# Residuals added straight from the two halves of a product's tile, and mixer products in pairs of 256 and 512 columns, in a fp32 decoder trunk

## The chip, the core and the metric

The kernel runs on one core of one Trainium2 chip. The metric is the device time of one execution, in microseconds; of three runs the median counts. The engines that matter here are TensorE (PE: matrix products; PEld is its loading of weights), VectorE (DVE), ScalarE (ACT) and SyncE (SP), which issues the DMAs. Each engine works through its own list of instructions in order, and waits there until what an instruction needs has been signalled by others.

## The reference

Two macaron layers on x of 256 tokens by 1024 features, in fp32; six sub-layers s = 0 to 5 follow each other:

```python
x = x + 0.5 * (1.0 + mod[:, 0, 2]) * swiglu(pre(x, 0), ffn_wi[l, 0], ffn_wo[l, 0])
h = pre(x, 1)                       # rmsnorm, scale and shift
y = hgrn2_mixer(...) if kind == 0 else diff_attention_mixer(...)   # ends in o @ w_out
x = x + (1.0 + mod[:, 1, 2]) * y
x = x + 0.5 * (1.0 + mod[:, 2, 2]) * swiglu(pre(x, 2), ffn_wi[l, 1], ffn_wo[l, 1])
```

So s = 0, 2, 3, 5 are SwiGLU feed-forward parts (1024 to 2 x 2816 and back), s = 1 is the HGRN2 mixer and s = 4 the differential attention. After every sub-layer a gate per feature multiplies its output, and the sum with x is the new x: this is the residual that the change touches.

## The kernel before

**Layout.** x is held transposed in SBUF, as `xT` of 128 partitions x 8 chunks x 256 tokens; chunk d holds features 128 d to 128 d + 127. Weights come from HBM in blocks of up to 1 MB (`raw`, three buffers, DMAs issued by SP in a fixed order, up to four blocks ahead). Each block is split into a high part on ACT (`whi`, L231) and the rest on DVE (`wlo`, L232), two instructions each, up to two blocks ahead of its use; inputs are split likewise (`xh`/`xl`, `hx`, `a`, `yh`/`yl`). A product of fp32 precision is then the sum of three products in PE's fast type: high x high, high x low and low x high.

**Two forms of a product.** `mm3` (L349) issues the three as three matmuls of 256 columns into one 256-wide sum (L351 to L353). `mm2` (L355) issues low-weight x high-input as 256 columns (L359) and high-weight x [high|low input] as one matmul of 512 columns (L360), into a tile of two halves whose sum is the result:

```python
PE.matmul(acc[:, :S], wl, x2[:, 0], ...)                              # L359
PE.matmul(acc, wh, x2.rearrange("p a s -> p (a s)"), ...)             # L360
```

`joined` (L362) adds the halves: ACT copies the right one to SBUF (L365, tile `post`), DVE adds the left one to it (L366). Products land in PSUM tiles `mm` of 512 columns; five buffers rotate, so a tile's first matmul waits until the tile five before it has been read.

**The output products.** A feed-forward part ends in `out_product`: chunks are taken two by two, each with 22 k-steps of `mm2`, then `residual(s, d, joined(acc))`. A mixer ends in `mixer_out`: 8 k-steps (one for each head's `yh`, `yl`) of `mm3` for each chunk. The first six steps of chunks 0 to 3 are fill for PE while the heads are still worked on; when the last head is done, steps 6 and 7 of these follow, then chunks 4 to 7 whole.

**The tail of a sub-layer.** `residual` is one instruction on DVE (L504, xT = mm x gate + xT), and then, unless it is the last sub-layer, `scaled_chunk` prepares the next sub-layer's input: ACT makes `xh` (L301), DVE `xl` (L302), ACT the square `sq`, and DVE adds it to `ss` (L313). After chunk 7's `ss`, a matmul with ones (L327, `finish_norm`) sums over partitions; ACT makes `rstd` of it. Meanwhile `in_first` multiplies the next sub-layer's first weights with the unnormed `xh`, `xl` chunks as they come (L351 to L353, 258 columns: two carry the shift), in several tiles at once, and applies `rstd` later. In the last sub-layer a DMA stores each chunk in place of that.

**Order.** The program is written in one order, and a scheduler then sets the order of each engine's list by costs of its own; a change at one place can move instructions around it.

Of the kernel before, what the change touches and what calls it, by code (L numbers as in the profile page):

```python
# [10 lines left out]
F32 = mybir.dt.float32  # L11
F32R = mybir.dt.float32r
I32 = mybir.dt.int32
U32 = mybir.dt.uint32
AF = mybir.ActivationFunctionType
ALU = mybir.AluOpType
AX = mybir.AxisListType

P = 128
S = 256  # L20
# [4 lines left out]
H = 8  # L25
# [75 lines left out]
def trunk(ctx: ExitStack, tc, xT_in, c_in, vecs, positions, lam_in, kc_in, ada_w, ffn_wi, ffn_wo,  # L101
# [348 lines left out]

    def mixer_out(s, yh, yl, late):

        ws = [get((s, "out", d)) for d in range(2)]
        todo = [(w, c * P) for w in ws for c in range(2)]
        acc = []
        for w, c0 in todo:
            acc.append(mm_tile())
            for k in range(H - 2):
                mm3(acc[-1][:, :S], w, k, c0, yh[k], yl[k], k == 0, False)
                if k == H // 2 - 2:  # L460
                    yield
            yield
        while late:
            yield
        shift_cols(s + 1)
        for d in range(KD):
            if d < 4:
                for k in (H - 2, H - 1):
                    mm3(acc[d][:, :S], todo[d][0], k, todo[d][1], yh[k], yl[k], False, k == H - 1)
                residual(s, d, acc[d])  # L470
                continue
            w = get((s, "out", d // 2))
            t = mm_tile()
            for k in range(H):
                mm3(t[:, :S], w, k, (d % 2) * P, yh[k], yl[k], k == 0, k == H - 1)
            residual(s, d, t)
# [26 lines left out]
    def residual(s, d, acc):  # L503
        V.scalar_tensor_tensor(out=xT[:, d], in0=acc[:, :S], scalar=mod_a["mod_g", s][:, d:d + 1], in1=xT[:, d],  # L504
                               op0=ALU.mult, op1=ALU.add)
        if s + 1 < NSUB:
            scaled_chunk(s + 1, d)
        else:
            nc.sync.dma_start(out=out[d * P:(d + 1) * P, :], in_=xT[:, d])
# [5 lines left out]
    def out_product(s, ws_of, K, y2):  # L515

        for dp in range(4):
# [10 lines left out]
            for c in range(2):  # L528
                residual(s, dp * 2 + c, joined(acc[c]))

# [40 lines left out]
    def hgrn2(s):  # L571
        with tc.tile_pool(name="hg", bufs=2, reuse_waits="tile") as hp, \
# [12 lines left out]
            V.tensor_scalar(out=lb1, in0=lb, scalar1=-1.0, scalar2=1.0, op0=ALU.mult, op1=ALU.add)  # L585
            yh = [yp.tile([P, S], F32R, name=f"yh{h}") for h in range(H)]
            yl = [yp.tile([P, S], F32R, name=f"yl{h}") for h in range(H)]

# [16 lines left out]
            def fill():  # L605
                for p in range(4):
# [24 lines left out]
                    for c in range(2):  # L631
                        sl = slice(c * S, (c + 1) * S)
                        active.append(lag(STAG * c, core)(2 * p + c, qg[:, sl], k_[:, sl], lf[:, sl], v[:, :, c],
                                           qg[:, 2 * S + c * S:2 * S + (c + 1) * S]))
                yield from mixer_out(s, yh, yl, active)

            def core(h, q, k_, lf, v, g):
# [94 lines left out]
                for t in range(2):  # L732
# [3 lines left out]
                                       op0=ALU.mult, op1=ALU.mult)  # L736
                split(yh[h], yl[h], rs)

# [59 lines left out]
    def diff_attention(s):  # L798
        with tc.tile_pool(name="at", bufs=2, reuse_waits="tile") as hp, \
# [14 lines left out]
            V.tensor_scalar(out=slg, in0=vec[:, V_SL:V_SL + 1], scalar1=1.0 - LAMBDA_INIT, scalar2=None, op0=ALU.mult)  # L814
            yh = [yp.tile([P, S], F32R, name=f"byh{h}") for h in range(H)]
            yl = [yp.tile([P, S], F32R, name=f"byl{h}") for h in range(H)]
            scale = DH ** -0.5

            def fill():
                pre = in_first(s, [(s, "in", 0, 1), (s, "in", 0, 0)])  # L820
                rs = [{} for _ in range(4)]
                for n, (p, st) in enumerate(B_ORDER):
# [21 lines left out]
                    if not st:  # L844
                        for c in range(2):
                            active.append(lag(STAGA * c, core)(2 * p + c, r, c))
                yield from mixer_out(s, yh, yl, active)

# [44 lines left out]
            def core(h, r, c):  # L893
# [59 lines left out]
                for t in range(2):  # L953
                    PE.transpose(pn[:, t * P:(t + 1) * P], on[:, t * P:(t + 1) * P], ident)
                A.activation(out=yh[h], in_=pn[:, :S], func=AF.Copy, scale=slg)
                V.scalar_tensor_tensor(out=yl[h], in0=pn[:, :S], scalar=slg, in1=yh[h].bitcast(F32),
                                       op0=ALU.mult, op1=ALU.subtract)
# [163 lines left out]
```

## Time and profile before

| | us |
|---|---|
| median of three runs | 1062.84 |
| lowest and highest of the three | 1062.73, 1063.62 |
| the profiled execution's own time | 1065.88 |
| the span of that profile | 1064.1 |

| engine | busy us | share of the span | instructions |
|---|---|---|---|
| PE | 1042.3 | 98% | 7200 |
| DVE | 882.3 | 83% | 1761 |
| ACT | 662.8 | 62% | 1258 |
| POOL | 3.8 | 0% | 20 |

A share is an average over the whole span. Whether time can be won at one place depends on which engine is waited for there. Times within the span count from its start. An instruction's duration on PE or DVE is longer than the distance to the next one's start where the two overlap, so costs in a row are read from starts. The profile's rows join instructions of one kind that follow each other (x3), with the time from the first's start to the last's end.

### The profile page before, as it was taken

How to read it: one execution, taken by the hardware profiler on the slowest of the kernel's cores; microseconds unless marked ns; L12 is line 12 of the kernel's file. 1: busy time of each engine (PE TensorE's matmuls, PEld its weight loads, DVE VectorE, ACT ScalarE, POOL GpSimd, SP SyncE). 2: the span in 40 equal slices, each digit the busy share in tenths (PEclk: the TensorE clock that was granted, in tenths of full speed). 3: DMA queues.
4: the chain of work that ended last, by engine and by line, in shares of the span. 5: the costliest groups of instructions: out<-in, count | busy, mean ns of one | idle time of the engine just before them, and what ended most of it. 6: DMA issues, size and time to landing. Idle time of an engine off the chain costs nothing.

```text
span 1064.1 us, 18510 instructions
## 1 busy us (share of the span) xinstructions
PE 1042.3 (98%) x7200; PEld 931.9 (88%) x7200; DVE 882.3 (83%) x1761; ACT 662.8 (62%) x1258; POOL 3.8 (0%) x20
## 2 busy tenths in 40 slices
PE   8999999998999999999999999999999999999998
PEld 6788888897898898888889888888999999888887
DVE  6899888699897699998668999976899979887653
ACT  5666655586876675656446556654678786565541
POOL 0000000000000000000000000000000000000000
PEclk9999999999999999999999999999999999999999
DMA  9988788566764158887654888985466725766560
GB/s 357 356 285 294 266 309 284 179 243 231 259 248 170 50 193 307 311 321 273 219 193 160 317 312 322 336 292 194 165 241 249 261 86 198 283 227 214 190 209 20
DMA packets 41160, 256.03 MB, mean 241 GB/s; under 512 B 4721, under 2 KB 7025, under 8 KB 13426
## 3 DMA queue, kind: packets, MB, share of 16 engines
q1 hardware_dynamic: 41074, 254.87, 66.7%
q8 instruction: 56, 0.92, 0.3%
q14 instruction: 30, 0.25, 0.1%
HBM read 253.80 MB, written 1.05 MB: 240 GB/s over the span
## 4 chain that ended last, share of the span: by engine, by line
PE 84%; DVE 7%; DMA 5%; ACT 4%; issue 1%; SPq 0%; DVEq 0%
PE mm L360 41%; PE mm L359 21%; PE mm L351 5%; PE mm L352 5%; PE mm L353 5%; DMA rawa<-in_ada_w_dram 3%; PE mm L420 2%; PE mm L418 1%; PE mm L419 1%; DVE rawa L180 1%; DVE wlo L232 1%; DMA raw<-in_a_w_in_dram 1%; ACT whi L231 1%; DMA raw<-in_ffn_wi_dram 1%; ACT L337 1%
## 5 line engine op out<-in xcount | busy, mean ns | idle before, releaser
L232 DVE TENSOR_TENSOR wlo<-raw,whi 128x1024 fp32r<-128x1024 f32 (+1 forms) x336 | 394.1, 1197 | 88.3 <-ACT whi L231 87.4
L231 ACT ACTIVATE whi<-raw 128x1024 fp32r<-128x1024 f32 (+1 forms) x336 | 335.0, 1032 | 118.3 <-issue 47.5
L360 PE MATMUL mm<-hx,whi 128*128 128x512 f32 x1152 | 407.2, 397 | 0.0
L359 PE MATMUL mm<-hx,wlo 128*128 128x256 f32 x1152 | 323.9, 281 | 0.5 <-DVE post L399 0.5
L360 PEld LDWEIGHTS mm<-hx,whi 128*128 128x128 f32 x1152 | 216.5, 188 | 53.0
L360 PE MATMUL mm<-a,whi 128*128 128x512 f32 x704 | 247.3, 393 | 0.0
L359 PEld LDWEIGHTS mm<-hx,wlo 128*128 128x128 f32 x1152 | 216.3, 188 | 1.5 <-PE aux L1001 0.8
L359 PE MATMUL mm<-a,wlo 128*128 128x256 f32 x704 | 199.1, 283 | 0.0
L360 PEld LDWEIGHTS mm<-a,whi 128*128 128x128 f32 x704 | 132.2, 188 | 30.5
L180 DVE CUSTOM_DVE_ANT_0 rawa<-rawa,cact 128x1024 f32<-128x1024 f32 x128 | 154.6, 1222 | 3.3 <-DMA rawa<-in_ada_w_dram 3.1
L365 ACT ACTIVATE post<-mm 128x256 f32<-128x256 f32 x176 | 67.3, 383 | 128.7 <-PE mm L360 127.2
L359 PEld LDWEIGHTS mm<-a,wlo 128*128 128x128 f32 x704 | 132.4, 188 | 0.0
L366 DVE TENSOR_TENSOR post<-mm,post 128x256 f32<-128x256 f32 x176 | 73.7, 423 | 34.2 <-ACT post L365 33.4
L353 PE MATMUL mm<-xh,wlo 128*128 128x258 f32 x288 | 81.2, 283 | 0.0
L352 PE MATMUL mm<-xl,whi 128*128 128x258 f32 x288 | 81.0, 283 | 0.0
L351 PE MATMUL mm<-xh,whi 128*128 128x258 f32 x288 | 80.8, 285 | 0.0
L418 PE MATMUL mm<-whi,hx 128*128 128x256 f32 x208 | 59.8, 287 | 0.0
L420 PE MATMUL mm<-wlo,hx 128*128 128x256 f32 x208 | 59.3, 285 | 0.0
L419 PE MATMUL mm<-whi,hx 128*128 128x256 f32 x208 | 58.8, 283 | 0.0
L512 ACT ACTIVATE a<-us 128x256 fp32r<-128x256 f32 x88 | 34.9, 412 | 32.5 <-DVE us L560 28.9
L352 PEld LDWEIGHTS mm<-xl,whi 128*128 128x128 f32 x288 | 54.5, 189 | 0.2
L353 PEld LDWEIGHTS mm<-xh,wlo 128*128 128x128 f32 x288 | 54.4, 189 | 0.1
(226 smaller groups left out, 1444.4 us busy)
## 6 DMA issues: line engine op xcount, KB each, us to landing
raw<-in_ffn_wi_dram SPq DMA_DIRECT2D x84, 1024.0 KB, 4.8
rawa<-in_ada_w_dram SPq DMA_DIRECT2D x64, 1024.0 KB, 4.9
raw<-in_ffn_wo_dram SPq DMA_DIRECT2D x32, 1024.0 KB, 5.0
raw<-in_a_w_in_dram SPq DMA_DIRECT2D x16, 1024.0 KB, 4.8
raw<-in_ffn_wo_dram SPq DMA_DIRECT2D x16, 768.0 KB, 4.2
raw<-in_b_w_in_dram SPq DMA_DIRECT2D x12, 1024.0 KB, 4.7
rawa<-in_ada_w_dram SPq DMA_DIRECT2D x16, 512.0 KB, 7.6
wq<-in_ffn_wi_dram SPq DMA_DIRECT2D x16, 256.0 KB, 7.6
```

Of the source, the lines that this page charges most:

```text
L180: V.tensor_tensor_reduce(out=self.raw[:, d], in0=self.raw[:, d], in1=cact, scale=1.0, scalar=0.0, op0=ALU.mult, op1=ALU.add, accum_out=sum ...
L231: pin(A.activation(out=self.hi[:, sl], in_=self.raw[:, sl], func=AF.Copy))
L232: pin(V.tensor_tensor(out=self.lo[:, sl], in0=self.raw[:, sl], in1=self.hi[:, sl].bitcast(F32), op=ALU.subtract))
L351: PE.matmul(acc, wh, rh, start=start, stop=False)
L352: PE.matmul(acc, wh, rl, start=False, stop=False)
L353: PE.matmul(acc, wl, rh, start=False, stop=stop)
L359: PE.matmul(acc[:, :S], wl, x2[:, 0], start=start, stop=False, skip_group_check=True)
L360: PE.matmul(acc, wh, x2.rearrange("p a s -> p (a s)"), start=False, stop=stop, skip_group_check=True)
L366: V.tensor_tensor(out=t, in0=acc[:, :S], in1=t, op=ALU.add)
L418: PE.matmul(acc, xh_, wh, start=k == 0, stop=False)
L419: PE.matmul(acc, xl_, wh, start=False, stop=False)
L420: PE.matmul(acc, xh_, wl, start=False, stop=k == KD - 1)
```

## The change

The residual becomes two instructions on DVE for every chunk: xT gets gate x right half added, then gate x left half, both read from PSUM. `joined` is no longer called by `out_product` (it stays in the other products that use it). The mixers' `y` of a head is one tile of two halves, and `mixer_out` uses `mm2` in place of `mm3`.

```diff
-    def mixer_out(s, yh, yl, late):
+    def mixer_out(s, y2, late):
@@
-                mm3(acc[-1][:, :S], w, k, c0, yh[k], yl[k], k == 0, False)
+                mm2(acc[-1], w, k, c0, y2[k], k == 0, False)
@@
-                    mm3(acc[d][:, :S], todo[d][0], k, todo[d][1], yh[k], yl[k], False, k == H - 1)
+                    mm2(acc[d], todo[d][0], k, todo[d][1], y2[k], False, k == H - 1)
@@
-                mm3(t[:, :S], w, k, (d % 2) * P, yh[k], yl[k], k == 0, k == H - 1)
+                mm2(t, w, k, (d % 2) * P, y2[k], k == 0, k == H - 1)
@@
     def residual(s, d, acc):
-        V.scalar_tensor_tensor(out=xT[:, d], in0=acc[:, :S], scalar=mod_a["mod_g", s][:, d:d + 1], in1=xT[:, d],
-                               op0=ALU.mult, op1=ALU.add)
+
+        for part in (acc[:, S:], acc[:, :S]):
+            V.scalar_tensor_tensor(out=xT[:, d], in0=part, scalar=mod_a["mod_g", s][:, d:d + 1], in1=xT[:, d],
+                                   op0=ALU.mult, op1=ALU.add)
@@
-                residual(s, dp * 2 + c, joined(acc[c]))
+                residual(s, dp * 2 + c, acc[c])
@@
-                split(yh[h], yl[h], rs)
+                split(y2[h][:, 0], y2[h][:, 1], rs)
@@
-                A.activation(out=yh[h], in_=pn[:, :S], func=AF.Copy, scale=slg)
-                V.scalar_tensor_tensor(out=yl[h], in0=pn[:, :S], scalar=slg, in1=yh[h].bitcast(F32),
+                A.activation(out=y2[h][:, 0], in_=pn[:, :S], func=AF.Copy, scale=slg)
+                V.scalar_tensor_tensor(out=y2[h][:, 1], in0=pn[:, :S], scalar=slg, in1=y2[h][:, 0].bitcast(F32),
```

In the four feed-forward parts (8 chunks each) 32 copies on ACT and 32 additions on DVE go and 32 residual instructions come; in the two mixers 16 residual instructions come, and 128 k-steps of three matmuls become pairs, 128 matmuls fewer. The residual's line is L504 before and L506 after.

Three places show how the lists of instructions differ. First DVE at the end of the HGRN2 mixer. Before:

```order
L504 SCALAR_TENSOR_TENSOR xT<-mm,mod_g,xT 128x256 x3
L232 TENSOR_TENSOR wlo<-raw,whi 128x1024 x2
L302 SCALAR_TENSOR_TENSOR xl<-xT,mod_a,xh 128x256 x2
L313 TENSOR_TENSOR ss<-ss,sq 128x256
L302 SCALAR_TENSOR_TENSOR xl<-xT,mod_a,xh 128x256
L313 TENSOR_TENSOR ss<-ss,sq 128x256
L504 SCALAR_TENSOR_TENSOR xT<-mm,mod_g,xT 128x256
L232 TENSOR_TENSOR wlo<-raw,whi 128x1024
L302 SCALAR_TENSOR_TENSOR xl<-xT,mod_a,xh 128x256
L313 TENSOR_TENSOR ss<-ss,sq 128x256
L232 TENSOR_TENSOR wlo<-raw,whi 128x1024
L504 SCALAR_TENSOR_TENSOR xT<-mm,mod_g,xT 128x256 x2
```

The same place after the change:

```order
L506 SCALAR_TENSOR_TENSOR xT<-mm,mod_g,xT 128x256 x3
L232 TENSOR_TENSOR wlo<-raw,whi 128x1024 x2
L302 SCALAR_TENSOR_TENSOR xl<-xT,mod_a,xh 128x256
L506 SCALAR_TENSOR_TENSOR xT<-mm,mod_g,xT 128x256 x3
L302 SCALAR_TENSOR_TENSOR xl<-xT,mod_a,xh 128x256
L313 TENSOR_TENSOR ss<-ss,sq 128x256
L506 SCALAR_TENSOR_TENSOR xT<-mm,mod_g,xT 128x256 x2
L232 TENSOR_TENSOR wlo<-raw,whi 128x1024
L302 SCALAR_TENSOR_TENSOR xl<-xT,mod_a,xh 128x256
L313 TENSOR_TENSOR ss<-ss,sq 128x256
L302 SCALAR_TENSOR_TENSOR xl<-xT,mod_a,xh 128x256
L313 TENSOR_TENSOR ss<-ss,sq 128x256
```

The eight residual instructions of the stretch are sixteen. With a and b for the two of a chunk, and chunks 0 to 7, they stand as 0a 1a 0b, then 1b 2a 3a, 2b 3b, 4a 5a 4b 5b, and 6a 7a 6b 7b: a chunk's second one never stands right behind its first. The rest of the stretch (8 `wlo`, 8 `xl`, 7 `ss`) is the same. The attention's end has the same form.

Second, PE at the same end: the matmul L327 over `ss` and what is around it, `in_first`'s matmuls. Before:

```order
L353 MATMUL mm<-xh,wlo 128x258
L351 MATMUL mm<-xh,whi 128x258
L352 MATMUL mm<-xl,whi 128x258
L353 MATMUL mm<-xh,wlo 128x258
L327 MATMUL aux<-ss,ones 128x256
L351 MATMUL mm<-xh,whi 128x258
L352 MATMUL mm<-xl,whi 128x258
```

After:

```order
L352 MATMUL mm<-xl,whi 128x258 x2
L353 MATMUL mm<-xh,wlo 128x258
L352 MATMUL mm<-xl,whi 128x258
L353 MATMUL mm<-xh,wlo 128x258
L352 MATMUL mm<-xl,whi 128x258
L353 MATMUL mm<-xh,wlo 128x258
L351 MATMUL mm<-xh,whi 128x258
L352 MATMUL mm<-xl,whi 128x258
L353 MATMUL mm<-xh,wlo 128x258
L327 MATMUL aux<-ss,ones 128x256
L353 MATMUL mm<-xh,wlo 128x258
```

Counted from `in_first`'s first matmul, L327 has 63 matmuls ahead of it before and 80 after, since the scheduler puts work on a fourth tile ahead of it. At the attention's end the counts are 58 and 80.

Third, the end of DVE's list, the last sub-layer. Before:

```order
L504 SCALAR_TENSOR_TENSOR xT<-post,mod_g,xT 128x256
L232 TENSOR_TENSOR wlo<-raw,whi 128x768 x2
L366 TENSOR_TENSOR post<-mm,post 128x256
L504 SCALAR_TENSOR_TENSOR xT<-post,mod_g,xT 128x256
L366 TENSOR_TENSOR post<-mm,post 128x256
L504 SCALAR_TENSOR_TENSOR xT<-post,mod_g,xT 128x256
```

After:

```order
L506 SCALAR_TENSOR_TENSOR xT<-mm,mod_g,xT 128x256 x4
L232 TENSOR_TENSOR wlo<-raw,whi 128x768 x2
L232 TENSOR_TENSOR wlo<-raw,whi 128x1024 x4
L506 SCALAR_TENSOR_TENSOR xT<-mm,mod_g,xT 128x256 x4
L232 TENSOR_TENSOR wlo<-raw,whi 128x768 x2
L506 SCALAR_TENSOR_TENSOR xT<-mm,mod_g,xT 128x256 x4
```

The addition of the halves is gone, and the last four stand as 6a 6b 7a 7b, so that here a chunk's second one does follow its first.

SP's and POOL's lists are the same before and after. PE's list in the HGRN2 mixer is nearly the same up to its output product; inside the attention, transposes and score products have moved by a few matmuls.

## Rows read from the trace of the kernel before

**Rows 1.** The page: busy time of the engines, and the granted clock in slices.

```profile
PE 1042.3 (98%) x7200; PEld 931.9 (88%) x7200; DVE 882.3 (83%) x1761; ACT 662.8 (62%) x1258; POOL 3.8 (0%) x20
...
PEclk9999999999999999999999999999999999999999
```

**Rows 2.** Windows, attention without its end: length, busy us by engine, clock, DMA.

```profile
762.00:862.00 100.00, 98.75 (x786) 91.78 (x786) 90.16 (x247) 77.91 (x209) 0.00 (x0) 1.00 0.59 211
```

**Rows 3.** Groups by line: count | busy us, mean ns | idle before, releaser.

```profile
L366 DVE TENSOR_TENSOR post<-mm,post 128x256 f32<-128x256 f32 x176 | 73.7, 423 | 34.2 <-ACT post L365 33.4
L365 ACT ACTIVATE post<-mm 128x256 f32<-128x256 f32 x176 | 67.3, 383 | 128.7 <-PE mm L360 127.2
...
L504 DVE SCALAR_TENSOR_TENSOR xT<-post,mod_g,xT 128x256 f32<-128x256 f32 x32 | 15.4, 483 | 0.7
...
L504 DVE SCALAR_TENSOR_TENSOR xT<-mm,mod_g,xT 128x256 f32<-128x256 f32 x16 | 7.0, 483 | 1.3 <-PE mm L353 1.3
```

**Rows 4.** Timeline of PE, HGRN2's output product: start us, us, instruction.

```profile
367.20 0.28 PE L351 MATMUL mm<-yh,whi 128*128 128x256 f32 x1
367.32 0.28 PE L352 MATMUL mm<-yl,whi 128*128 128x256 f32 x1
367.43 0.28 PE L353 MATMUL mm<-yh,wlo 128*128 128x256 f32 x1
367.55 0.28 PE L351 MATMUL mm<-yh,whi 128*128 128x256 f32 x1
```

**Rows 5.** Timeline of PE, the attention's output product.

```profile
871.56 0.28 PE L351 MATMUL mm<-byh,whi 128*128 128x256 f32 x1
...
871.92 0.29 PE L351 MATMUL mm<-byh,whi 128*128 128x256 f32 x1
```

**Rows 6.** Timeline of PE, pairs in the last feed-forward part's output product.

```profile
1055.06 0.28 PE L359 MATMUL mm<-a,wlo 128*128 128x256 f32 x1
...
1055.77 0.28 PE L359 MATMUL mm<-a,wlo 128*128 128x256 f32 x1
...
1056.11 0.28 PE L359 MATMUL mm<-a,wlo 128*128 128x256 f32 x1
...
1057.52 0.28 PE L359 MATMUL mm<-a,wlo 128*128 128x256 f32 x1
```

**Rows 7.** Timeline of DVE, the end of HGRN2.

```profile
366.69 1.27 DVE L504 SCALAR_TENSOR_TENSOR xT<-mm,mod_g,xT 128x256 f32<-128x256 f32 x3 [0.61 <-PE mm L353]
...
382.99 0.43 DVE L313 TENSOR_TENSOR ss<-ss,sq 128x256 f32<-128x256 f32 x1
383.32 1.23 DVE L232 TENSOR_TENSOR wlo<-raw,whi 128x1024 fp32r<-128x1024 f32 x1
```

**Rows 8.** Timeline of PE, the first matmuls of `in_first` and L327 there.

```profile
376.03 0.28 PE L351 MATMUL mm<-xh,whi 128*128 128x258 f32 x1
...
376.39 0.29 PE L351 MATMUL mm<-xh,whi 128*128 128x258 f32 x1
...
383.64 0.60 PE L327 MATMUL aux<-ss,ones 128*128 128x256 f32 x2
```

**Rows 9.** Timeline of DVE, the end of the attention.

```profile
879.17 0.43 DVE L313 TENSOR_TENSOR ss<-ss,sq 128x256 f32<-128x256 f32 x1
```

**Rows 10.** Timeline of PE, L327 at that end.

```profile
879.96 0.59 PE L327 MATMUL aux<-ss,ones 128*128 128x256 f32 x2
```

**Rows 11.** Timeline, the last three instructions of ACT and DVE.

```profile
1060.18 0.39 ACT L365 ACTIVATE post<-mm 128x256 f32<-128x256 f32 x1 [1.73 <-PE mm L360]
1060.60 0.42 DVE L366 TENSOR_TENSOR post<-mm,post 128x256 f32<-128x256 f32 x1 [1.16 <-ACT post L365]
1061.06 0.48 DVE L504 SCALAR_TENSOR_TENSOR xT<-post,mod_g,xT 128x256 f32<-128x256 f32 x1
```

**Rows 12.** Timelines of DVE and PE, the end of the first feed-forward part.

```profile
212.50 0.42 DVE L313 TENSOR_TENSOR ss<-ss,sq 128x256 f32<-128x256 f32 x1
...
213.54 0.59 PE L327 MATMUL aux<-ss,ones 128*128 128x256 f32 x2
```

More of the change, by code (lines that the diff above doesn't have):

```diff
@@ L585, in hgrn2 @@
             V.tensor_scalar(out=lb1, in0=lb, scalar1=-1.0, scalar2=1.0, op0=ALU.mult, op1=ALU.add)
-            yh = [yp.tile([P, S], F32R, name=f"yh{h}") for h in range(H)]
-            yl = [yp.tile([P, S], F32R, name=f"yl{h}") for h in range(H)]
+            y2 = [yp.tile([P, 2, S], F32R, name=f"y{h}") for h in range(H)]
             def t2(name, n=2 * S, bufs=2):
@@ L634, in fill @@
                                            qg[:, 2 * S + c * S:2 * S + (c + 1) * S]))
-                yield from mixer_out(s, yh, yl, active)
+                yield from mixer_out(s, y2, active)
             def core(h, q, k_, lf, v, g):
@@ L814, in diff_attention @@
             V.tensor_scalar(out=slg, in0=vec[:, V_SL:V_SL + 1], scalar1=1.0 - LAMBDA_INIT, scalar2=None, op0=ALU.mult)
-            yh = [yp.tile([P, S], F32R, name=f"byh{h}") for h in range(H)]
-            yl = [yp.tile([P, S], F32R, name=f"byl{h}") for h in range(H)]
+            y2 = [yp.tile([P, 2, S], F32R, name=f"by{h}") for h in range(H)]
             scale = DH ** -0.5
@@ L846, in fill @@
                             active.append(lag(STAGA * c, core)(2 * p + c, r, c))
-                yield from mixer_out(s, yh, yl, active)
+                yield from mixer_out(s, y2, active)
             def prep_qk(src, r, key):
```

## The prediction

> **What bounds the kernel now.** I read the page's busy times first, then the engines' timelines at each place where the changed lines run. PE is busy for 98% of the span, and its granted clock is at the top of the scale in all 40 slices, the higher of its two levels (2.4 GHz) [rows 1]. So PE's stream of matmuls sets the time nearly everywhere, and work on DVE or ACT counts only where PE waits for it. The groups by line say the same of what the change removes: L365 on ACT costs 383 ns and L366 on DVE 423 ns, 176 times each, and the wait in front of L365 is for PE (127.2 of 128.7 us) [rows 3]. ACT and DVE are waiting for PE there and not the other way round. Three places are left where the output's way through DVE can be late: the two mixers' ends, where DVE has a queue of its own, and the last chunk, where nothing follows that hides it.
>
> **The pairs.** A k-step of three matmuls takes PE from 367.20 to 367.55 us, 0.35 us [rows 4], in the attention 0.36 us [rows 5]. The pair that replaces it has the same 768 columns, and seven such steps take 1055.06 to 1057.52 us, 0.351 us each, single ones 0.34 [rows 6]. So 128 matmuls fewer bring PE nothing that these rows show: the columns are what is paid for. Bounds: no gain at all, and 64 x 0.01 + 64 x 0.02 = 1.9 us if every step took 0.34. I take zero, from the mean of the seven, which are the same instruction form. The Trainium skill, TensorE: Matmul & The Clock Gate, "Back-to-back issue gap", gives columns over the clock plus some 2.5 ns for each matmul; by that one matmul less for each step would be 128 x 2.5 ns = 0.3 us, and the sum below would be 0.3 us lower.
>
> **The feed-forward parts.** Each of their 32 chunks loses 383 ns of ACT and 423 ns of DVE and gets 483 ns of DVE (a residual from PSUM takes as long as one from SBUF: 483 and 483) [rows 3]. A chunk is ready earlier: DVE no longer waits for ACT's copy. At the ends of s = 0, 2 and 3 that is worth nothing. The last `ss` of s = 0 ends at 212.50 + 0.42 = 212.92 us, and L327 starts at 213.54 [rows 12], 0.6 us later, since PE has not got through what stands ahead of it; the other two ends read alike. What would be earlier is waited for by nobody. The cover here is `in_first`'s stream of matmuls; if it were gone, the chain would be shorter by the copy, so this is no place for a loss. I take zero.
>
> **The last chunk.** Here the chain is bare: copy at 1060.18, addition at 1060.60, residual from 1061.06 to 1061.54 [rows 11], 1.36 us. After the change two residuals follow each other, the second needing the first's result. What such a need costs on DVE can be read here: the addition ends at 1061.02 and the residual starts 0.04 us later. So the first lasts 0.48, the gap is 0.04, and the second lasts 0.48: 1.00 us. **-0.36 us**. The store behind it is the same.
>
> **The end of HGRN2.** Here DVE is what is late. It starts on the residuals at 366.69 us and goes without a gap to the last `ss`, 382.99 + 0.43 = 383.42 us [rows 7]. L327 on PE follows at 383.64 [rows 8], 0.22 us after. The change puts eight more residuals into this run and takes nothing out of it, because the mixers never called `joined`. Three residuals that don't need each other take 1.27 us [rows 7], so they start (1.27 - 0.48)/2 = 0.394 us apart. In the new list a chunk's second residual never stands right behind its first, so I take that price: 8 x 0.394 = 3.15 us. The last `ss` then ends at 386.57 us.
>
> PE does not lose all of that, since the scheduler has put more of `in_first` ahead of L327: 80 matmuls in place of 63. A matmul of 258 columns costs 0.36/3 = 0.12 us [rows 8], so 17 of them cover 2.04 us, and without a wait L327 would start at 383.64 + 2.04 = 385.68. It waits until 386.57 and about 0.05 more for the signal: **+0.9 us** that PE stands still. I looked for earlier waits on the way. Chunk 5's product starts at 367.55 [rows 4] and needs the buffer of chunk 0, whose second residual is third in the list and ends at 366.69 + 1.27 = 367.96: some 0.4 us of wait. Chunk 4's second residual, eleven instructions later, is needed in the same way by `in_first`'s second tile. These waits come before L327 and are not added to it: PE arrives later and then waits less, as long as they stay below 0.9 us together with the waits for `xl`.
>
> **The end of the attention.** The same eight residuals, 3.15 us. The last `ss` ends at 879.17 + 0.43 = 879.60 [rows 9] and moves to 882.75. L327 starts at 879.96 [rows 10], and 22 more matmuls stand ahead of it (80 for 58), 2.64 us, so without a wait it would be at 882.60. PE waits 0.15 us, with the signal **+0.2 us**.
>
> After L327 the matmuls that were moved ahead are missing as cover for `rstd`. The tiles that wait for it still have the fifth tile's work in front; I take zero, and 1 us at each end as the bound, half of the 2.04 us of cover that was moved.
>
> **What the scheduler moved elsewhere.** In the attention some transposes and score products stand elsewhere. No row prices that. In its 100 us PE is idle for 1.25 us by the windows view [rows 2]; I take zero and that much on both sides.
>
> **Sum.** 0.9 + 0.2 - 0.36 = +0.75 us. The profiled execution took 1065.88 us, 3 us over the median of 1062.84; by the sum it would be 1066.6, and against the median **1063.6 us**. A measurement of this kernel can tell about 0.2%, 2.1 us, from no change (the three runs spread by 0.9 us), so the forecast is that no difference is seen.
>
> **Rivals.**
> - **The mixers' ends pay more for each residual (slower).** If a residual waited for the whole of the one in front, the step would be 0.48 + 0.04 = 0.52 us in place of 0.394, as between the last two instructions of the kernel [rows 11]. Eight of these add 1.0 us to each end, and as L327 waits for DVE at both, all of it counts: +0.75 + 2.0 = +2.75, 1065.6 us. It is slower by over 0.2% from about +0.7 us for each end on. Against it: the row of three at 1.27 us, with the same form and the same PSUM source [rows 7]. Chance 0.07. Without the gap, at 0.483 from start to start, eight add 8 x 0.09 = 0.7 us to each end: +2.15, 1065.0 us, chance 0.03, as the same row speaks against it. The Trainium skill, VectorE: DVE Perf Modes, "The DRAIN you can't avoid", has this as a rule: the next instruction starts only when the one before has emptied the pipe, so their number is to be kept low.
> - **The attention's moved instructions, or the cover after L327, cost a wait (slower).** Heads and output product are tied together; 1.25 us for the one and 1 us for the other give +0.75 + 2.25 = +3.0, 1065.8 us. Against: the order on PE is close to the old one. Chance 0.12, of which 0.07 lie above 1065.0.
> - **The pairs stream faster, or fewer waits (faster).** All steps at 0.34 would give -1.9 + 0.75 = -1.2, 1061.7 us, if PE's time in the heads' fill is on the path; at the two ends DVE decides and a faster PE only waits longer. The move in the attention may also gain up to 1.25 us. Chance 0.17, nearly all still within 0.2%.
> - **The feed-forward ends gain after all.** If the weights' splitting, which shares ACT and DVE with the removed copies, lets later DMAs start sooner and PE waits less, each of the 32 chunks could be worth its part of ACT's 383 ns; by the rows PE never waits there, and a gain of over 2.1 us needs one. Chance 0.06, 1060 us.
>
> **How the numbers follow.** The forecast, 1062.6 to 1064.6 us, has 0.55. The rest is 0.10 + 0.12 above and 0.17 + 0.06 below. The range that leaves out 2 in 10: down to 1061.6 (the pairs' bound) and up to 1065.8 (the dearer residuals and the cover). Slower by over 0.2% (above 1065.0): 0.07 + 0.07 and 0.02 for what I haven't seen, 0.16. Faster by over 0.2% (below 1060.7): 0.06. Within: 0.78.
>
> **What would show it.** The last three instructions become two, 1.0 us after PE's last matmul instead of 1.36. At HGRN2's end the residuals start 0.39 us apart and the last `ss` starts 3.1 us later against the first residual (19.4 in place of 16.3 us); L327 stands 10.6 us behind `in_first`'s first matmul if PE was not held at chunk 5. In the attention the same, with L327 at about 9.8 us (80 x 0.12 + 0.2). The pair of a mixer's product takes 0.35 us. The forecast is wrong if residuals there start 0.48 us or more apart, if PE's wait at L327 is over 2 us, or if a pair takes another time than a triple. Gaps on PE inside the attention that the old trace lacks would put the cause there.

## The result: slower by 0.55%

| | median us | runs | ratio to the kernel before |
|---|---|---|---|
| before | 1062.80 | 4 | |
| changed | 1070.09 (1067.92 to 1071.06) | 4 | 1.0055, 95% interval 1.0042 to 1.0068 |
| changed, once more, beside 1064.32 us for the kernel before | 1070.59 (1068.74 to 1072.74) | 5 | 1.0062, 1.0046 to 1.0078 |

The forecast was 1063.6 us, with 1061.6 to 1065.8 as its range. The result lies above that range, and its interval excludes no change. The profiled execution of the changed kernel took 1069.82 us (span 1067.9 us).

The page of the changed kernel, busy time of the engines and the granted clock in slices, against [rows 1]:

```profile
PE 1043.7 (98%) x7072; PEld 924.8 (87%) x7072; DVE 888.8 (83%) x1777; ACT 650.3 (61%) x1226; POOL 3.8 (0%) x20
...
PEclk9999999999999999999999999999999999999999
```

PE has 128 matmuls less and is busy for 1.4 us more; nothing here names a place. The waits do. I asked for the waits view of PE in the changed kernel twice, from the end of HGRN2's output product to 430 us and from the end of the attention's to 930 us. Both answers are these two lines (what waited for what, us in total, times, longest):

```profile
PE mm L359 <- DVE wlo L232: 1.9, 1, 1.9
PE mm L351 <- ACT xh L301: 0.2, 1, 0.2
```

The wait of 1.9 us is not at L327, where the prediction put one, but 21.6 us behind it. At L327 itself PE does not wait at all: the last `ss` ends 0.5 us ahead of it, and the matmuls before it run up to it without a gap. The timeline of PE in the changed kernel shows both L327 and the matmul that waited (start us, us, instruction, idle time before it and its releaser), first HGRN2, then the attention:

```profile
384.63 0.59 PE L327 MATMUL aux<-ss,ones 128*128 128x256 f32 x2
...
406.24 0.36 PE L359 MATMUL mm<-hx,wlo 128*128 128x256 f32 x1 [1.94 <-DVE wlo L232]
...
884.58 0.59 PE L327 MATMUL aux<-ss,ones 128*128 128x256 f32 x2
...
906.19 0.36 PE L359 MATMUL mm<-hx,wlo 128*128 128x256 f32 x1 [1.94 <-DVE wlo L232]
```

The distance is 21.61 us both times. What DVE does in it, by its timeline in the changed kernel behind HGRN2's L327:

```profile
386.22 0.88 DVE L486 SCALAR_TENSOR_TENSOR hn<-xT,mod_a,rstd 128x256 f32<-128x256 f32 x2 [0.96 <-ACT rstd L345]
...
400.32 0.76 DVE L515 TENSOR_TENSOR a<-us,a 128x256 fp32r<-128x256 f32 x2
401.00 1.22 DVE L180 CUSTOM_DVE_ANT_0 rawa<-rawa,cact 128x1024 f32<-128x1024 f32 x1
402.14 0.08 DVE L180 DVE_READ_ACCUMULATOR2_ANT sums<- 128x1 f32 x1
402.14 1.22 DVE L180 CUSTOM_DVE_ANT_0 rawa<-rawa,cact 128x1024 f32<-128x1024 f32 x1
...
404.08 0.87 DVE L564 SCALAR_TENSOR_TENSOR us<-post,col,gs 128x256 f32<-128x256 f32 x2
404.87 1.22 DVE L232 TENSOR_TENSOR wlo<-raw,whi 128x1024 fp32r<-128x1024 f32 x1
```

`rstd` comes from L327, by way of ACT; behind it DVE goes through `hn`, `hx`, the scaled tiles and two dot products of an adaLN block (L180; adaLN makes scale, shift and gate of a sub-layer from the condition, and this block is for the gate of the sub-layer that has just begun) without a gap to 406.09 us, where the first half of the low part `wlo` of a weight block is done. PE waits for exactly that.

### The profile page after: what moved, and what is told of

The parts are those of the page before. It is cut to its first block, busy times and chain, and to the rows that moved or that the text cites. A ratio compares the mean times of both kernels' runs of the same rounds, so it can differ in the third digit from the quotient of the medians.

```text
span 1067.9 us, 18260 instructions
## 1 busy us (share of the span) xinstructions
PE 1043.7 (98%) x7072; PEld 924.8 (87%) x7072; DVE 888.8 (83%) x1777; ACT 650.3 (61%) x1226; POOL 3.8 (0%) x20
## 4 chain that ended last, share of the span: by engine, by line
PE 77%; DVE 12%; DMA 5%; ACT 5%; issue 1%; DVEq 0%; SPq 0%
PE mm L360 42%; PE mm L359 22%; DVE wlo L232 3%; DMA rawa<-in_ada_w_dram 2%; PE mm L351 2%; PE mm L352 2%; PE mm L353 2%; DVE rawa L180 2%; ACT whi L231 1%; PE mm L418 1%; PE mm L420 1%; PE mm L419 1%; DMA raw<-in_a_w_in_dram 1%; DVE hx L494 1%; DVE hn L486 1%
## 5 line engine op out<-in xcount | busy, mean ns | idle before, releaser
L180 DVE CUSTOM_DVE_ANT_0 rawa<-rawa,cact 128x1024 f32<-128x1024 f32 x128 | 153.7, 1216 | 0.0
L365 ACT ACTIVATE post<-mm 128x256 f32<-128x256 f32 x144 | 54.8, 382 | 93.8 <-PE mm L360 92.6
L366 DVE TENSOR_TENSOR post<-mm,post 128x256 f32<-128x256 f32 x144 | 59.6, 418 | 20.6 <-ACT post L365 19.8
L351 PEld LDWEIGHTS mm<-xh,whi 128*128 128x128 f32 x288 | 53.7, 189 | 1.4 <-ACT xh L301 0.8
L506 DVE SCALAR_TENSOR_TENSOR xT<-mm,mod_g,xT 128x256 f32<-128x256 f32 x96 | 43.0, 478 | 14.2 <-PE mm L360 13.3
```

What stands on the lines that cost most here:

```text
L180: V.tensor_tensor_reduce(out=self.raw[:, d], in0=self.raw[:, d], in1=cact, scale=1.0, scalar=0.0, op0=ALU.mult, op1=ALU.add, accum_out=sum ...
L351: PE.matmul(acc, wh, rh, start=start, stop=False)
L366: V.tensor_tensor(out=t, in0=acc[:, :S], in1=t, op=ALU.add)
```

## The experiments

Theory A: VectorE's queue is what costs, eight more residuals at each mixer's end. Rival B: the products in pairs cost, since their long matmul needs both halves of a head's y. All experiments were timed beside runs of the kernel before on the same chip. Behind `in_first`, the function `in_two` multiplies the next weight blocks with the normed input `hx`, in pairs, 16 matmuls to a tile. In the text, "third tile" is the start of the third of these tiles behind a mixer, the waiting matmul of the rows above.

### Which part costs: the residuals or the pairs

**The changed kernel once more.**

> The changed kernel once more, beside the others of this call. Theory A (VectorE's queue): from a mixer's first residual to a weight block's low part some 20 us behind L327 VectorE is what everything waits for, so eight more residuals at 0.394 us cost their whole 3.15 us at each mixer's end, and PE stands still for about 2 us in front of that block. Rival B (the pairs): the loss comes from the products in pairs, whose long matmul needs both halves of a head's y. Both expect +4 to +8 us on the kernel before here, a PE wait of about 2 us for wlo some 21 us behind each mixer's L327, and the granted clock below 1.

Measured: 1.0062 (1.0046 to 1.0078), the two waits again, 21.63 us behind L327 both times. The profiled execution had the clock at 1.00 to the end of its work, so the waits come without the fall of the clock that was expected; more of it below.

**The feed-forward part alone.** `mixer_out` is as before, `residual` gets a count of halves:

```diff
-    def residual(s, d, acc):
+    def residual(s, d, acc, halves=1):
+        for part in (acc[:, S:], acc[:, :S])[2 - halves:]:
...
-                residual(s, dp * 2 + c, joined(acc[c]))
+                residual(s, dp * 2 + c, acc[c], 2)
```

> Only the feed-forward parts get the two residuals; the mixers keep triples and one residual. A and B: -0.36 us from the last chunk, so -0.2 to -0.6 us on the kernel before, no PE wait of 2 us behind the mixers, clock 1.0. If HGRN2's heads are still done some 2.5 us earlier, as in the changed kernel, that gain is not the pairs'.

Measured: 1062.93 us, 0.9990 (0.9981 to 0.9999), -1.4 us by the medians, more than the 0.2 to 0.6 expected, with an interval that holds both. There is a wait for the same `wlo` behind HGRN2, 0.9 us, and none behind the attention. The wait belongs to this execution: a weight block landed there 6.7 us after its issue, where the blocks before and behind it took 4.8 to 5.0, ACT's `whi` waited for it and DVE for ACT; the kernel with the change in the attention alone (below) has the same HGRN2 end, no such landing and no such wait.

**Triples kept, two residuals.** In the mixers:

```diff
-        for part in (acc[:, S:], acc[:, :S])[2 - halves:]:
+        for part in (acc[:, S:] if halves == 2 else acc[:, :S], acc[:, :S]):
```

> Triples kept in the mixers, but each of their chunks gets two residuals, both of the left half (so gate times the product is added twice there); feed-forward parts as in the change. A: 16 more residuals at 0.394 us, +5 to +6.5 us on the run with the feed-forward part of the change alone, PE waits of 1 to 3 us for wlo behind both mixers. B: like that run, within 1 us of it.

Measured: 1069.22 us, 1.0045 (1.0032 to 1.0058); 6.3 us above the run before this one. L327 to the third tile is 21.62 us at both ends.

**Pairs, one residual.** The changed kernel with

```diff
-        for part in (acc[:, S:], acc[:, :S]):
+        for part in (acc[:, S:], acc[:, :S])[2 - halves:]:
```

> Pairs in the mixers as in the change, but one residual for each of their chunks (the right half, high weight times low y, is left out); feed-forward parts as in the change. A: no PE wait for wlo behind the mixers, and the time of the run with the feed-forward part alone or up to 3 us less, if the pairs are what made HGRN2's heads end earlier. B: as slow as the changed kernel, +4 us or more on the kernel before.

Measured: 1064.16 us, 0.9994 (0.9985 to 1.0002), 1.2 us above the feed-forward part alone; a wait of 0.2 us for the `wlo` is left behind HGRN2. So the four kernels form a square: the second residual costs 6.3 us with triples and 1070.59 - 1064.16 = 6.4 us with pairs; pairs cost 1.2 to 1.4 us with either, at the edge of what these runs resolve. The two profiles, both with the clock at 1.00, show none of that: their spans are 1061.0 us with pairs and 1061.6 with triples. Rival B has fallen: the residuals in the mixers are the cost.

### One end at a time

In the changed kernel, `mixer_out` takes `mm3` for the other mixer, whose chunks get one residual:

```diff
+        pair = s in (1,)        # (4,) in the second kernel
+        def step(acc, w, k, c0, start, stop):
+            if pair:
+                mm2(acc, w, k, c0, y2[k], start, stop)
+            else:
+                mm3(acc[:, :S], w, k, c0, y2[k][:, 0], y2[k][:, 1], start, stop)
...
-        for part in (acc[:, S:], acc[:, :S]):
+        for part in (acc[:, S:], acc[:, :S])[1 if s in (1, 4) and s not in (1,) else 0:]:
```

> The feed-forward part of the change, and pairs with two residuals in HGRN2 alone; the attention keeps triples and one residual. Theory A (VectorE's queue): one end's eight residuals, +2.5 to +3.2 us on the run with the feed-forward part alone, one PE wait of about 2.1 us for wlo behind HGRN2's L327 and none behind the attention's. Rival B (only the attention's form costs, or a fall of the clock that both ends together bring): under +1 us.

> The feed-forward part of the change, and pairs with two residuals in the attention alone. Theory A: +2.5 to +3.2 us on the run with the feed-forward part alone, one PE wait of about 2.1 us for wlo behind the attention's L327, none that long behind HGRN2's. The costs of this and of the run with HGRN2 alone add up to that of the whole change, 6 to 8 us on the run with the feed-forward part alone.

Measured: HGRN2 alone 1066.35 us, 1.0023 (1.0014 to 1.0032); the attention alone 1066.65 us, 1.0025 (1.0016 to 1.0034). Each has one wait of 1.9 us for `wlo`, 21.61 us behind the L327 of its own mixer, and none behind the other. Against the feed-forward part alone, by ratios, that is +0.0033 and +0.0035 of 1064.3 us, 3.5 and 3.7 us, a little over what was expected. Together 7.2 us, where the whole change costs 0.0072 x 1064.3 = 7.7 us: within their intervals of some 1 us and more the two ends add up. These two kernels ran on another chip than the four of the square, so the ratios are compared and not the times.

### Is it the length of VectorE's queue?

The changed kernel without the eight `xl` at each mixer's end (`scaled_chunk` leaves L302 out where `low` is false):

```diff
-            scaled_chunk(s + 1, d)
+            scaled_chunk(s + 1, d, low=s not in (1, 4))
```

> The changed kernel, but at the two mixers' ends the eight low parts xl (L302) are left out, so in_first multiplies stale ones: eight instructions of 0.394 us go from VectorE's queue where eight residuals came. Theory A: the queue is as long as before, so 6 us less than the changed kernel, within 1.5 us of the run with the feed-forward part alone, and no PE wait of 2 us for wlo. Rival C (what costs is that a chunk's xT is done later, after its second residual, and what hangs on it): less than 3 us better than the changed kernel, and the waits of PE stay.

Measured: 1066.01 us, 1.0016 (1.0007 to 1.0025), 0.0046 x 1064.3 = 4.9 us better than the changed kernel and 0.0026 x 1064.3 = 2.8 us worse than the feed-forward part alone. Both expectations missed, and the waits tell why. The waiting matmul behind the attention, by the timeline of PE in this kernel (lines stand one further on):

```profile
880.03 0.38 PE L328 MATMUL aux<-ss,ones 128*128 128x256 f32 x1
...
901.62 0.36 PE L360 MATMUL mm<-hx,wlo 128*128 128x256 f32 x1 [1.29 <-DVE wlo L232]
```

DVE has the eight instructions less, and its last `ss` of this end is done at 879.17 us, 0.9 us ahead of L327; but the scheduler has left 75 matmuls ahead of L327, where the triples with one residual had 58. PE gets there late by its own list, and the 17 matmuls are missing behind it; behind HGRN2, with 75 for 63, the wait is 1.29 us as well. Again the third tile starts 21.59 us behind L327. So theory A, that only the length of the queue up to L327 counts, has fallen in that form. What stays the same in every one of these kernels is the chain behind L327.

### The chain behind L327

I wrote the theory anew (A2 in the expectations below): DVE needs 21.6 us from L327 to that `wlo`, whatever was before it; PE needs less when matmuls were put ahead of L327, and waits for the difference. It can be tested by shortening the chain and leaving everything up to L327 as it is. The first adaLN block, whose two dot products stand in front of the `wlo`, is moved two weight blocks on in the list that `plan` makes:

```diff
-            lim, skip = (n - 12, 3) if j != 1 else (n - 8, 3)
+            lim, skip = (n - 12, 5 if s in (2, 5) else 3) if j != 1 else (n - 8, 3)
```

> The changed kernel, with the first adaLN block of the two sub-layers behind the mixers placed two weight blocks later in the list of blocks, so that VectorE splits the weight block PE waits for ahead of two dot products of 1.14 us (L180) instead of behind them. Theory A2 (behind L327 a fixed chain of some 21.5 us on VectorE ends in that block's wlo, and PE has only 19.6 us of work left for it, because the matmuls put ahead of L327 are missing there): the chain is 2.3 us shorter, both waits of 2.1 us go or fall under 0.3 us, -3.5 to -4.2 us on the changed kernel. Rival D (VectorE is late as a whole, whatever it does first): the waits come back behind the next block, and the gain is under 1 us.

Measured: 1065.04 us, 1.0008 (0.9999 to 1.0018): 0.0054 x 1064.3 = 5.7 us better than the changed kernel, more than the 3.5 to 4.2 expected, and both waits are gone. The two profiles, both with a mean clock of 1.00, differ in span by 1066.3 - 1062.5 = 3.8 us, as expected. From the first residual to L327 nothing has moved: 20.64 and 20.62 us, for 20.67 and 20.65. The same stretch of DVE's timeline in this kernel:

```profile
400.72 0.76 DVE L515 TENSOR_TENSOR a<-us,a 128x256 fp32r<-128x256 f32 x2
401.38 2.36 DVE L232 TENSOR_TENSOR wlo<-raw,whi 128x1024 fp32r<-128x1024 f32 x2
...
408.85 1.22 DVE L180 CUSTOM_DVE_ANT_0 rawa<-rawa,cact 128x1024 f32<-128x1024 f32 x1
```

and PE's, L327 and the third tile:

```profile
385.07 0.38 PE L327 MATMUL aux<-ss,ones 128*128 128x256 f32 x1
...
404.58 0.28 PE L359 MATMUL mm<-hx,wlo 128*128 128x256 f32 x1
```

The third tile starts 19.51 us behind L327 with no wait: that is PE's own work there. Rival D, a wait that comes back behind the next block, is out: PE has no wait over 0.3 us behind L327 up to 450 us.

| kernel | matmuls ahead of L327: HGRN2, attention | L327 to the third tile, us |
|---|---|---|
| before (first profile) | 63, 58 | 21.69, 22.13 |
| before (second profile) | 63, 58 | 23.12 (late DMA), 22.13 |
| feed-forward part alone | 63, 58 | 22.60 (late DMA), 22.13 |
| pairs, one residual | 66, 62 | 21.55, 21.68 |
| without `xl` | 75, 75 | 21.59, 21.59 |
| triples, two residuals | 80, 80 | 21.62, 21.62 |
| changed | 80, 80 | 21.61, 21.61 |
| changed, dots later | 80, 80 | 19.51, 19.51 |
| feed-forward part alone, dots later | 63, 58 | 21.55, 22.13 |

PE's own work is 19.51 us with 80 matmuls ahead, 21.55 with 63 (17 x 0.12 = 2.04 more) and 22.13 with 58 (22 x 0.12 = 2.64 more, 22.15). DVE's chain is 21.6. The kernel before had 0.0 and 0.5 us to spare: behind HGRN2 its PE was already at the edge of a wait.

### Versions meant to beat both

**The feed-forward part alone, dots later.**

> The feed-forward part of the change alone, with the same two adaLN blocks placed later. A2: the wait of 1.07 us for wlo behind HGRN2 goes, the attention's end had none: -0.5 to -1.2 us on the run with the feed-forward part alone, about 2 us under the kernel before. D: no gain. Against it: the adaLN block is then split later, and its transfer meets others.

Measured: 1062.42 us, 0.9985 (0.9976 to 0.9995); no wait on PE behind either mixer. It has the lowest ratio of the kernels tried, 1.9 us under the kernel before by the medians.

This run also says what the later block does not mend. Both kernels with the dots later ran beside the same runs of the kernel before, and the changed one is still 1065.04 - 1062.42 = 2.6 us slower, with no wait behind L327 in either (spans 1062.5 and 1059.8 us). From the first residual of a mixer's end to the next `out_product` it takes 136.26 us behind HGRN2 and 136.24 behind the attention, for 134.61 and 135.31: +1.65 and +0.93. That is what DVE's longer queue costs PE ahead of L327. So of the 7.7 us by which the changed kernel stands above the feed-forward part alone, some 5 hung on the place of the two dot products, and 2.6 stay.

**The kernel before, dots later.**

> The kernel before, with the first adaLN block of the two sub-layers behind the mixers placed two weight blocks later, and nothing of the change. A2: the kernel before has a wait of up to 1.4 us for the same wlo behind HGRN2 where the mixer ends early, and none behind the attention, so 0 to -1 us on the kernel before; the rest of what the run with both edits gains on it (1.9 us) is the feed-forward part's. If this run alone gains all of it, the feed-forward part is worth only the 0.36 us of the last chunk or less.

Measured: 1063.46 us, 0.9989 (0.9980 to 0.9998). By the ratios the block's place alone brings 1.2 us, the feed-forward part alone 1.1 us and both 1.6 us; the intervals of some 1 us on either side allow that they add up, and that they don't.

**The feed-forward part alone, with the sums of squares on GpSimd.**

> The feed-forward part of the change alone, with the seven additions to ss at each mixer's end on GpSimd instead of VectorE. A2: VectorE's run up to L327 is 7 x 0.336 = 2.35 us shorter, and if GpSimd's last addition comes no later than VectorE's did, L327 is up to 2 us earlier and up to 1 us is gained behind HGRN2. If one GpSimd addition takes over 1.5 us, L327 waits for it and the run is 1 to 3 us slower than with the feed-forward part alone.

```diff
-            V.tensor_tensor(out=ss, in0=ss, in1=sq, op=ALU.add)
+            add.tensor_tensor(out=ss, in0=ss, in1=sq, op=ALU.add)     # nc.gpsimd at the mixers' ends
```

Measured: 1069.55 us, 1.0052 (1.0039 to 1.0065), 6.6 us worse than the feed-forward part alone. The group of these additions in this kernel, and behind it PE's timeline at its longest wait in HGRN2's end and at L327:

```profile
L313 POOL TENSOR_TENSOR ss<-ss,sq 128x256 f32<-128x256 f32 x14 | 12.7, 909 | 537.2 <-ACT sq L312 536.7
```

```profile
375.67 0.39 PE L352 MATMUL mm<-xl,whi 128*128 128x258 f32 x1 [1.15 <-DVE xl L302]
...
381.06 0.70 PE L327 MATMUL aux<-ss,ones 128*128 128x256 f32 x2 [0.88 <-POOL ss L313]
```

An addition takes 909 ns there (times on POOL are rough in these profiles) for 422 on DVE, below the 1.5 us that I had named as the limit, and the kernel loses all the same: the scheduler gave DVE and PE another order, in which PE now waits for an `xl` as well. A shorter queue on one engine is no gain if the order is made anew around it. Which of the new waits costs how much was not separated.

### The kernel before, profiled again

> The kernel before, profiled a second time. In its first profile ACT waits at 252.9 us for a weight block that landed 7.3 us after its issue, and HGRN2's output product starts some 2.2 us later than in the run with the feed-forward part of the change alone. If that was a chance of the one execution, this profile has no such landing, a span near 1062 us, and the output product at about 336 us. If it belongs to the kernel, it is here again, and the feed-forward part of the change gains about 2 us there.

Measured: 0.9999 (0.9990 to 1.0008), as it must be; HGRN2's output product starts at 335.92 us, 2.4 us earlier than in the first profile. So the late landing belonged to that execution, and the gain of some 2 us that the traces show in HGRN2 for the changed kernel is none of the change. The second profile gave the time back within 70 us: PE's clock is at 0.50 for 3.4 us from 363.6 us on, and a weight block comes late behind the mixer, so that PE waits 1.4 us for the same `wlo`. The ends are therefore compared below between two profiles that start HGRN2's output product within 1.1 us of each other (335.04 and 336.12 us).

## Why the prediction was wrong

The two profiles to compare are the changed kernel (second profile) and the feed-forward part alone, both with the clock at 1.00 in these stretches. The first residual of a mixer's end on DVE and the first matmul of the next `out_product` on PE; in the changed kernel:

```profile
363.43 0.48 DVE L506 SCALAR_TENSOR_TENSOR xT<-mm,mod_g,xT 128x256 f32<-128x256 f32 x1 [0.60 <-PE mm L360]
...
502.14 0.28 PE L359 MATMUL mm<-a,wlo 128*128 128x256 f32 x1
...
862.31 0.48 DVE L506 SCALAR_TENSOR_TENSOR xT<-mm,mod_g,xT 128x256 f32<-128x256 f32 x1 [0.66 <-PE mm L360]
...
1000.74 0.28 PE L359 MATMUL mm<-a,wlo 128*128 128x256 f32 x1
```

and with the feed-forward part alone:

```profile
364.52 0.48 DVE L505 SCALAR_TENSOR_TENSOR xT<-mm,mod_g,xT 128x256 f32<-128x256 f32 x1 [0.61 <-PE mm L353]
...
500.48 0.28 PE L359 MATMUL mm<-a,wlo 128*128 128x256 f32 x1
...
860.81 0.48 DVE L505 SCALAR_TENSOR_TENSOR xT<-mm,mod_g,xT 128x256 f32<-128x256 f32 x1 [0.68 <-PE mm L353]
...
996.10 0.28 PE L359 MATMUL mm<-a,wlo 128*128 128x256 f32 x1
```

HGRN2's end takes 138.71 us in place of 135.96, +2.75; the attention's 138.43 in place of 135.29, +3.14. The prediction had +0.9 and +0.2, and 3.15 us for the eight residuals on DVE at each. DVE's price was right; that PE's 17 and 22 matmuls would cover two thirds and more of it was wrong. The feed-forward part's profile has the late landing behind HGRN2 in it. The kernel with the change in the attention alone has the same HGRN2 end without it:

```profile
364.17 0.48 DVE L513 SCALAR_TENSOR_TENSOR xT<-mm,mod_g,xT 128x256 f32<-128x256 f32 x1 [0.61 <-PE mm L353]
...
499.15 0.28 PE L359 MATMUL mm<-a,wlo 128*128 128x256 f32 x1
```

That is 134.98 us, and against it HGRN2's end takes 3.73 us more. So nearly the whole price on DVE, and at HGRN2 somewhat more, came through at both ends.

Point by point:

- **The pairs: right.** Eleven steps of HGRN2's product in the changed kernel, from 370.13 to 373.97 us, take 0.349 us each; a triple took 0.35 [rows 4]. The square of experiments leaves them 1.2 to 1.4 us, where the steps alone would give nothing; the spans of the two profiles do not show that remainder either, and its cause stays open. The 0.3 us that the prediction worked out from the Trainium skill (TensorE: Matmul & The Clock Gate, "Back-to-back issue gap", which gives the 2.5 ns for an isolated matmul) are below what these runs resolve.
- **The feed-forward parts: about right, with a wrong reading.** "The other two ends read alike" does not hold. L327 comes 0.6 us behind the last `ss` at the end of s = 0 only; at the end of s = 2 the kernel before has

```profile
568.47 0.42 DVE L313 TENSOR_TENSOR ss<-ss,sq 128x256 f32<-128x256 f32 x1
568.68 0.28 PE L352 MATMUL mm<-xl,whi 128*128 128x258 f32 x1
568.94 0.48 PE L327 MATMUL aux<-ss,ones 128*128 128x256 f32 x1
```

  so L327 follows the end of `ss` by 0.05 us and the matmul before it by 0.26 in place of 0.12: PE waits 0.14 us for DVE. The end of s = 3 reads the same. In the changed kernel the last `ss` is 1.1 us ahead of L327 at all three ends. From the first matmul of the output product of s = 2 to that of s = 3 the kernel before takes 187.2 us and the changed one 187.1, so each of the two ends gained 0.14 us that the prediction took as zero.
- **The last chunk: right.** The last instruction of the changed kernel on DVE is the two residuals, 1.00 us as forecast:

```profile
1064.34 1.00 DVE L506 SCALAR_TENSOR_TENSOR xT<-mm,mod_g,xT 128x256 f32<-128x256 f32 x2 [1.10 <-PE mm L360]
```

- **The price of a residual on DVE: right.** In the changed kernel the rows behind [rows 7] are these; four of them take 1.65 us, (1.65 - 0.48)/3 = 0.39 us from start to start, and the rival with 0.52 us for each is out:

```profile
363.85 1.30 DVE L506 SCALAR_TENSOR_TENSOR xT<-mm,mod_g,xT 128x256 f32<-128x256 f32 x3 [1.01 <-PE mm L360]
...
379.88 1.65 DVE L506 SCALAR_TENSOR_TENSOR xT<-mm,mod_g,xT 128x256 f32<-128x256 f32 x4
...
383.71 0.41 DVE L313 TENSOR_TENSOR ss<-ss,sq 128x256 f32<-128x256 f32 x1
```

  The last `ss` starts 19.86 us behind the first residual, where 19.4 was forecast; 0.2 us of it is a wait for ACT's `whi`. The Trainium skill's rule that was named with that rival (VectorE: DVE Perf Modes, "The DRAIN you can't avoid", an instruction starts when the one before has emptied the pipe) is taken back in part by the same section: an instruction that is not held back starts earlier. The trace agrees with that for residuals that don't need each other; where the second needs the first, as in the last chunk, it starts behind the first's end, 1.00 us for the two.
- **PE up to L327: too small by 0.8 us at each end.** From the first residual to L327 the changed kernel takes 20.67 us at HGRN2 (16.94 with the feed-forward part alone), less 2.04 for the matmuls moved ahead: +1.69 in place of +0.9. At the attention 20.65 for 17.05, less 2.64: +0.96 in place of +0.2. PE's waits for buffers, 0.57 and 0.32 us in front of chunks 5 and 6 of HGRN2, came as forecast for chunk 5; some 0.7 us more went in `in_first` at each end, the longest piece of it (0.4 us) for ACT's `xh` of a chunk that DVE had finished later. The prediction let all of these be swallowed by one wait at L327 as long as they stayed below 0.9 us. At HGRN2 they sum to more; at the attention it had no more than 0.2 us there to swallow them; and there is no wait at L327 in either. So this term was mis-sized as well: the kernels with the dots later give it as 1.65 and 0.93 us.
- **Behind L327: this step failed.** "The tiles that wait for it still have the fifth tile's work in front; I take zero, and 1 us at each end as the bound." It is 2.1 us of standing still at each end (1.06 more than the feed-forward part alone has behind HGRN2, 2.11 more behind the attention). I had counted the matmuls moved ahead of L327 as cover for DVE's longer queue, and priced their absence behind L327, against the 21.6 us of DVE's work that L327 lets loose, at nothing. Moving them only chooses where PE stands. I looked for what follows L327 in the tiles waiting for `rstd` and not in the weight block behind them, and missed that PE had 0.5 us to spare there at the attention's end and none at HGRN2's.

The sum with these terms, for the two profiles: 2.75 + 3.14 = 5.9 us. The spans differ by 1066.3 - 1061.6 = 4.7, since HGRN2 started its end 1.1 us earlier in the one and 0.2 us were won between the mixers. Without the late landing the sum is 3.73 + 3.14 = 6.9. The rival with the cover after L327 named the mechanism, with a chance of 0.12 for all it held and 1 us for the cover, where the bound in the text was 1 us at each end; the cover cost 1.06 + 2.11 us by these profiles and 2.11 at each without the late landing. None of the signs that the prediction listed for being wrong came: the residuals start 0.39 us apart, L327 has no wait, a pair takes as long as a triple. The list did not look behind L327.

## The granted clock

The changed kernel's runs stand higher against the feed-forward part alone than the ends explain: 0.0072 by ratio is 7.7 us, the ends are 5.9, or 6.9 without the late landing. The intervals of the two ratios leave that open, but the granted clock differs too. In the changed kernel's first profile PE's clock falls twice; the windows view (length, then PE, PEld, DVE, ACT, POOL busy, clock, DMA share, GB/s):

```profile
359.00:362.80 3.80, 1.69 (x9) 1.02 (x8) 1.29 (x3) 1.89 (x6) 0.00 (x0) 1.00 0.00 0
362.80:366.20 3.40, 3.40 (x13) 2.86 (x12) 2.17 (x5) 1.93 (x3) 0.00 (x0) 0.50 0.02 5
...
403.00:407.10 4.10, 2.16 (x13) 1.64 (x12) 4.10 (x12) 1.07 (x3) 0.00 (x0) 1.00 0.72 230
407.10:410.50 3.40, 3.40 (x13) 2.91 (x12) 3.40 (x6) 2.00 (x2) 0.00 (x0) 0.51 0.54 164
```

Both times PE has just stood still, at the end of HGRN2's heads and in front of the third tile, and then runs at the lower level (1.2 GHz, 0.50) for 3.4 us, which costs it 1.7 us of work. The first of the two places is not the change's: the kernel before has the same fall in its second profile. The wait in front of the third tile is the change's own. The profiles of the changed kernel, of triples with two residuals and of the two kernels with one end hold eight such waits of 1.9 to 2.0 us; at three of them the clock falls for 3.4 us (from 407.15 us here, 906.52 with triples, 901.39 with the attention alone), at five it doesn't, in the second profile of the changed kernel at neither. No profile has a fall there without such a wait.

Over the runs, the kernel before had a mean clock of 1.000 in 12 of the 21 that were timed beside the changed kernel (median 1063.3 us) and less in the others (1065.0); the changed kernel 1.000 in one of five (1068.7) and 0.996 to 0.998 in four (1069.5 to 1072.7). At 1.000 the two kernels are 5.4 us apart, with one run on the one side, near the 5.9 of the ends less the last chunk's 0.36. By the mean clocks, the lower level took 2.6 us from the changed kernel's five runs and 1.2 from the eleven of the feed-forward part alone, an estimate from (1 - clock) x span. So the clock can account for some 1.4 us of the 7.7; it is not shown. Against a simple rule stands the changed kernel with the dots later, which has no such wait and 1.000 in 2 of 11 runs. Why a fall follows one wait and not the next, no run here shows.

## What to carry to other kernels

When an edit lengthens an engine's queue and a scheduler moves other work in front of the wait, ask from where that work was taken: cover moved ahead of one wait is missing at the next, and the bound is the chain from the shared signal (here L327) to the end of what it lets loose, compared with the other engine's work in the same stretch. Look for that chain's end in the trace at the first place where the waiting engine has no slack, even 20 us on. And before folding work into the engine that is not the bound on average, count its queue stage by stage: taking 32 copies off ACT and 32 additions off DVE for 32 residuals brought about 1 us, and 16 instructions more on DVE cost 6 us.

## Not expected of the hardware

An addition of 128x256 numbers in fp32 took 909 ns on GpSimd and 422 ns on VectorE. A wait of PE of about 2 us came with 3.4 us at half the clock in one execution and with none in another of the same kernel.
